# Squares of four row tiles written into PSUM banks instead of activation tiles, in a Hymba-style decoder layer

## The chip, the cores and the metric

The kernel runs on one core of a Trainium2 chip. The metric is the device time of one execution in microseconds (us). A core has five engines that run beside each other: PE (TensorE: matmuls and weight loads), DVE (VectorE), ACT (ScalarE), POOL (GpSimd) and SP (SyncE, which here issues most of the DMAs). Tiles lie in SBUF or, for what PE produces, in eight PSUM banks of 128 partitions by 512 fp32 values.

## The reference

One layer of a hybrid decoder: 256 tokens of width 2048, all in fp32.

```python
u = rmsnorm(h, ln1)
# one projection, then an RG-LRU group (8 blocks) and a retention group (8 heads)
h = h + concat(A, B) @ W_out                         # 2048 -> 2048
u = rmsnorm(h, ln2)
ff = silu(u @ w_ffn_gate) * (u @ w_ffn_up)           # 2048 -> 5632, twice
h = h + ff @ w_ffn_down                              # 5632 -> 2048
return rmsnorm(h, final_norm_w)
```

The last norm needs the sum of the squares of every row of the final `h` (2048 values of each of 256 tokens). That sum is what the changed lines compute for the left half of the columns.

## The kernel before, in words

**Arithmetic.** Every fp32 product is made of three matmuls of a rounded type: each operand is split into a high part (a cast on ACT, line 123: `wh`, `bh`, `ah`, `sh`) and a rest (a subtraction on DVE, line 124: `wl`, `bl`, `al`, `sl`), and `three` (lines 683 to 685) issues high times high, high times low and low times high. A weight block that comes in by DMA is a tile `raw` of 128x1024; splitting it costs one cast and one subtraction of that size.

**Blocks and quads.** The feed-forward part runs in blocks. Each of the two down blocks (`down_block(0)` and `down_block(1)`) produces 1024 of the 2048 output columns, as four sums `c11`, `c12`, `c21`, `c22` (first digit: token half `t`, second digit: column half), one PSUM bank each. It goes through 22 quads, each a pair of 128-row slices of the inner dimension against a 2x2 arrangement of weights `b11, b12, b22, b21`. A plain quad takes eight products (24 matmuls). A summed quad takes seven, in Strassen's manner: `p1, p5, p6, p7` go into banks of their own, and DVE first forms sums of the raw weights (line 661, four 128x512 additions in place) that are split once more as `t1, t3` and `t2, t4`. In a summed quad `b11` is split into activation tiles (`bh`, `bl`) and not into weight tiles. Block 0 ends with its last two quads taken bank by bank; the quads of block 1 begin with 0 (plain), 12 (summed), 1 (plain), 19 (summed).

**Activation tiles.** `act_tile` hands out 128x512 tiles from one pool of 60 (`acts`, `bufs=60`). A request waits until some tile of the pool is no longer read by anyone. The left operands of the down blocks, `dl[i]`, live in this pool from the beginning of block 0 to their use in block 1: `ah` and `al` for each of 22 quads, and `sh` and `sl` for those whose quad is summed. At the start of block 1, `sh` and `sl` are still needed for nine quads (5, 7, 9, 11, 12, 13, 15, 17, 19), and for two of these, 12 and 19, they lie in another pool (`BESIDE`).

**PSUM.** Two pools of four banks, `bank` and `aux`; `room` gives one to the `c` sums and the other to the `p` sums of a block, and block by block they change places. Block 0 has its four `c` in `bank`, block 1 its four `c` in `aux` and its `p` in `bank`: the banks in which the `c` of block 0 stand are those of the `p` of block 1.

**After a sum.** When a `c` of block 0 is complete, DVE adds it to the residual rows (`htok`, line 945), and `down_post` squares the rows on ACT with an accumulated sum per row (line 983). The square itself, `junk`, is read by nobody; the accumulated sum `ssq` is what is kept. For these tiles a multiplication by the norm's weight (line 988, DVE) follows, deferred by 13 to 16 steps of the program.

**Order.** The kernel is written as a list of steps, with loads three half quads ahead. A planner puts the instructions of all engines into queues by its own timeline: an instruction goes into its engine's queue when its operands and the tiles it needs are free in that plan, the earlier one in the program first. On the chip each engine's queue is then fixed. Only the last step of block 1 has its PE order written out by hand.

Of the kernel before, what the change touches and what calls it, by code (L numbers as in the profile page):

```python
# [45 lines left out]
def tile_hymba_layer(ctx: ExitStack, tc: tile.TileContext, A: dict, out: bass.AP):  # L46
# [18 lines left out]
    def nm(s):  # L65
        counter[0] += 1
        return f"{s}_{counter[0]}"

    def act_tile(name, dt=F32):
        return apool.tile([P, 512], dt, tag="act", name=nm(name))  # L70
# [169 lines left out]
    def defer(steps, f):  # L240
        later.append([steps, f])
# [664 lines left out]
    def make_left(p):  # L906
        if dl[p] is None:
            place = sum_tile if p in BESIDE else act_tile
            dl[p] = Left(ff[p], p in EARLY_DOWN + SUMMED_DOWN[0] + SUMMED_DOWN[1], place)

    def down_block(d, ahead):
        ps = {} if d else ahead.ps

        def tile_of(c):
            return 2 * d + int(c[2]) - 1, int(c[1]) - 1

        def into(c, a, b=None, op=ALU.add):

            h = htok[tile_of(c)]
            t = a  # L920
            if b is not None:
                t = act_tile("part")
                v.tensor_tensor(out=t, in0=a, in1=b, op=ALU.subtract)
            v.tensor_tensor(out=h, in0=h, in1=t, op=op)
            return t

        def post(c):
            if c == "p1":
                ps["a1"] = act_tile("part")
                act.copy(out=ps["a1"], in_=ps[c])  # L930
                into("c11", ps["a1"])
            elif c == "p7":
                n = act_tile("n")
                v.tensor_tensor(out=n, in0=ps["p6"], in1=ps["a1"], op=ALU.subtract)
                into("c12", n, ps["p5"])
                m = into("c21", n, ps["p7"], ALU.subtract)
                into("c22", m, ps["p5"])
            elif c[0] == "c":
                cb, t = tile_of(c)
                if d and c[:3] == "c22":  # L940
                    c0 = S * (c == "c22b")
                    down_post(cb, t, c0, S, ps[c][:, c0 : c0 + S])
                else:
                    h = htok[cb, t]
                    v.tensor_tensor(out=h, in0=ps[c], in1=h, op=ALU.add)
                    down_post(cb, t, 0, 512)

        n = FT // 2
        quads = []
        for i in ORDER_DOWN[d]:  # L950
            if d == 0 and i in EARLY_DOWN:
                quads.append(Direct(ahead.shared[EARLY_DOWN.index(i)]))
            else:
                quads.append(Quad(A["w_down"][d * n + i], i in SUMMED_DOWN[d], lambda i=i: make_left(i)))
            quads[-1].pair = i
        if d:
            quads[-1].apart = quads[-2].apart = True
        tail = [("c11", 0, 512), ("c12", 0, 512), ("c21", 0, 512)]
        def half_over():
            h = htok[3, 1][:, S:]  # L960
            act.copy(out=h, in_=ps["c22"][:, S:])
            v.tensor_tensor(out=ps["c22b"][:, S:], in0=ps["c22b"][:, S:], in1=h, op=ALU.add)

        early = {}
        if d:

            early["c22"] = lambda: v.tensor_tensor(out=ps["c22"], in0=ps["c22"], in1=htok[3, 1], op=ALU.add)
            early["c22b"] = half_over
            tail[:0] = [("c22b", S, S, slice(0, 1))]
            tail += [("c22", 0, S), ("c22b", S, S, slice(1, 4))]  # L970
        else:
            tail.append(("c22", 0, 512))

        block(NB + 2 + d, quads, dl, post, ps, tail, early=early, ordered=d == 1)

    def down_post(cb, t, c0, cw, src=None):

        h = htok[(cb, t)][:, c0 : c0 + cw]
        src = h if src is None else src
        f = fw[cb][:, c0 : c0 + cw]  # L980
        n = cb + (c0 > 0)
        j = act_tile("junk")
        act.activation(out=j[:, :cw], in_=src, func=AF.Square, accum_out=ssq[:, t, n : n + 1])
        p = pre[:, t : t + 1]
        if cb < 3:
            if cb < 2:

                defer(13 + 2 * cb + t, lambda: v.tensor_tensor(out=h, in0=h, in1=f, op=ALU.mult))
                return
            pool.tensor_tensor(out=h, in0=h, in1=f, op=ALU.mult)  # L990
            if cb == 2:
                if t == 0:
                    act.activation(out=warm, in_=ssq[:, t, n : n + 1], func=AF.Sqrt)
                v.tensor_reduce(out=p, in_=ssq[:, t, :3], axis=mybir.AxisListType.X, op=ALU.add)
                v.tensor_scalar(out=p, in0=p, scalar1=1.0 / D, scalar2=EPS, op0=ALU.mult, op1=ALU.add)
            return
        if c0 + cw < 512:
            v.tensor_scalar(out=p, in0=ssq[:, t, n : n + 1], scalar1=1.0 / D, scalar2=p, op0=ALU.mult, op1=ALU.add)
            v.tensor_tensor(out=h, in0=src, in1=f, op=ALU.mult)
            return  # L1000

        q, r, w = ssq[:, t, n : n + 1], r3[:, t : t + 1], m3[:, t : t + 1]
        act.activation(out=r, in_=q, func=AF.Sqrt, scale=1.0 / D, bias=p)
        v.tensor_scalar(out=w, in0=q, scalar1=1.0 / D, scalar2=p, op0=ALU.mult, op1=ALU.add)
        v.tensor_tensor(out=h, in0=src, in1=f, op=ALU.mult)
        v.reciprocal(out=r, in_=r)
        v.tensor_scalar(out=w, in0=w, scalar1=-0.5, scalar2=r, op0=ALU.mult, op1=ALU.mult)
        v.tensor_scalar(out=w, in0=w, scalar1=r, scalar2=1.5, op0=ALU.mult, op1=ALU.add)
        rw = rw3[:, t : t + 1]
        pool.tensor_tensor(out=rw, in0=r, in1=w, op=ALU.mult)  # L1010
        rows = out[t * P : t * P + P, :]
        for c in (0, 1, 3, 2):
            z = htok[(c, t)]
            if c == 1:
                act.activation(out=z, in_=z, func=AF.Copy, scale=rw)
            elif c == 2 and t:
                v.tensor_scalar(out=z[:, :S], in0=z[:, :S], scalar1=r, scalar2=w, op0=ALU.mult, op1=ALU.mult)
                act.activation(out=z[:, S:], in_=z[:, S:], func=AF.Copy, scale=rw)
            else:
                e = pool if c == 2 else v  # L1020
                e.tensor_scalar(out=z, in0=z, scalar1=r, scalar2=w, op0=ALU.mult, op1=ALU.mult)
            (act if c % 2 and t else nc.sync).dma_start(out=rows[:, c * 512 : c * 512 + 512], in_=z)
# [128 lines left out]
    for step, (units, run) in enumerate(program):  # L1151
        need += sum(un.n_loads for un in units)
        while done < min(len(loads), need + AHEAD):
            un, j = loads[done]
# [109 lines left out]
```

## Time and profile before

| | |
|---|---|
| time, median of 3 runs | 1084.82 us (1084.63 to 1085.21) |
| the profiled execution's own time | 1085.53 us |
| its span, first to last instruction | 1083.7 us |
| PE busy | 1072.3 us, 99% |
| DVE busy | 972.0 us, 90% |
| ACT busy | 666.9 us, 62% |
| POOL busy | 56.5 us, 5% |
| mean granted TensorE clock | 0.996 |

The profile describes one execution. A group line gives a source line, an engine, an operation, output and inputs, the count, the busy time and mean of one, and after the bar the idle time of the engine just before such instructions and what ended it. In a timeline, the row's first number is the start in us from the beginning of the span, the second the duration; what stands in brackets is how long the engine had been idle before and which instruction released it. A window row gives for each engine the busy time and the number of instructions, and then the granted clock of TensorE (1.00 is full speed), the share of the DMA engines and their rate. The chain that ended last is 94% PE.

### The profile page before, as it was taken

The numbers are of one execution on the slowest core, as the hardware profiler recorded it, in microseconds if no ns is written. First come the engines' busy times: TensorE is split into PE (matmuls) and PEld (weight loads), VectorE is DVE, ScalarE is ACT, GpSimd is POOL, SyncE is SP. The second block draws the span as 40 slices with busy tenths as digits, with TensorE's granted clock in tenths as the row PEclk, the third lists the DMA queues.
The fourth block names the chain that finished last, engine by engine and source line by source line (L and its number), as shares of the span: only waits on it lengthen the run. The fifth ranks groups of instructions, "written<-read, shape, count | busy, mean of one in ns | idle before, by whom it ended". The sixth has DMA issues, their size and how long they took to land.

```text
span 1083.7 us, 14591 instructions
## 1 busy us (share of the span) xinstructions
PE 1072.3 (99%) x5083; PEld 897.5 (83%) x5083; DVE 972.0 (90%) x1411; ACT 666.9 (62%) x951; POOL 56.5 (5%) x73
## 2 busy tenths in 40 slices
PE   9999999999999999999999999999999999999997
PEld 7888888888888888888888888888888888878886
DVE  7789889988878889989999999999999899999886
ACT  7756744468746676656656566565656666655463
POOL 0603230000000000000000000000000010000001
PEclk9999999999999999999999999999999999999998
DMA  9964574554557587677776777776777856557662
GB/s 328 351 211 154 176 252 168 181 176 165 185 194 236 188 306 277 227 242 247 257 269 229 250 262 238 265 269 227 251 249 228 273 170 219 194 174 240 208 214 78
DMA packets 71386, 244.62 MB, mean 226 GB/s; under 512 B 8208, under 2 KB 8592, under 8 KB 71312
## 3 DMA queue, kind: packets, MB, share of 16 engines
q1 hardware_dynamic: 68400, 236.34, 64.3%
q0 software_dynamic: 1472, 4.72, 1.3%
q10 hardware_dynamic: 1440, 2.62, 0.6%
q8 instruction: 40, 0.66, 0.2%
q14 instruction: 34, 0.28, 0.1%
HBM read 239.46 MB, written 4.19 MB: 225 GB/s over the span
## 4 chain that ended last, share of the span: by engine, by line
PE 94%; POOL 1%; DMA 1%; DVE 1%; issue 1%; ACT 1%; SPq 0%; POOLq 0%; ACTq 0%
PE c L683 22%; PE c L685 22%; PE c L684 22%; PE fm L194 10%; PE fm L196 5%; PE tm L174 2%; PE tm L176 2%; PE tm L175 2%; PE p L685 1%; PE p L684 1%; PE p L683 1%; POOL sumsq L310 1%; PE ft L868 1%; DMA raw<-in_w_lx 1%; DMA raw<-in_w_v 0%
## 5 line engine op out<-in xcount | busy, mean ns | idle before, releaser
L123 ACT CAST wh<-raw 128x1024 fp32r<-128x1024 f32 (+1 forms) x500 | 464.5, 960 | 321.6 <-PE c L685 127.3
L124 DVE TENSOR_TENSOR wl<-raw,wh 128x1024 fp32r<-128x1024 f32 (+1 forms) x500 | 543.1, 1114 | 73.0 <-ACT wh L123 71.2
L684 PE MATMUL c<-wl,ah 128*128 128x512 f32 x814 | 317.7, 390 | 0.0
L685 PE MATMUL c<-wh,al 128*128 128x512 f32 x814 | 314.9, 389 | 0.0
L683 PE MATMUL c<-wh,ah 128*128 128x512 f32 x814 | 276.8, 392 | 0.0
L683 PEld LDWEIGHTS c<-wh,ah 128*128 128x128 f32 x814 | 153.4, 188 | 31.8 <-ACT wh L123 0.3
L685 PEld LDWEIGHTS c<-wh,al 128*128 128x128 f32 x814 | 152.8, 188 | 31.7 <-DVE al L124 0.3
L684 PEld LDWEIGHTS c<-wl,ah 128*128 128x128 f32 x814 | 152.9, 188 | 31.3
L194 PE MATMUL fm<-u,wh 128*128 128x512 f32 x512 | 161.3, 396 | 0.0
L196 PEld LDWEIGHTS fm<-u,wl 128*128 128x128 f32 x512 | 96.0, 188 | 22.5
L196 PE MATMUL fm<-u,wl 128*128 128x256 f32 x512 | 100.9, 278 | 0.0
L661 DVE TENSOR_TENSOR raw<-raw,raw 128x512 f32<-128x512 f32 x118 | 81.1, 688 | 2.0
L661 DVE TENSOR_TENSOR raw<-raw 128x512 f32<-128x512 f32 x118 | 80.6, 686 | 1.1
L194 PEld LDWEIGHTS fm<-u,wh 128*128 128x128 f32 x512 | 78.3, 189 | 0.3
L684 PE MATMUL c<-wl,sh 128*128 128x512 f32 x194 | 75.2, 389 | 0.0
L685 PE MATMUL c<-wh,sl 128*128 128x512 f32 x194 | 74.0, 389 | 0.0
L683 PE MATMUL c<-wh,sh 128*128 128x512 f32 x194 | 68.7, 391 | 0.3 <-ACT sh L123 0.3
L175 PE MATMUL tm<-wl,u 128*128 128x512 f32 x128 | 48.8, 394 | 0.0
L176 PE MATMUL tm<-wh,u 128*128 128x512 f32 x128 | 48.5, 390 | 0.0
L174 PE MATMUL tm<-wh,u 128*128 128x512 f32 x128 | 47.1, 398 | 0.8 <-ACT u L298 0.8
L1119 POOL DMA_DIRECT2D htok<-kept_rows x8 | 4.3, 546 | 796.4 <-DVE wl L124 704.0
L683 PEld LDWEIGHTS c<-wh,sh 128*128 128x128 f32 x194 | 36.4, 188 | 8.2 <-ACT sh L123 0.7
(247 smaller groups left out, 1076.2 us busy)
## 6 DMA issues: line engine op xcount, KB each, us to landing
raw<-in_w_gu SPq DMA_DIRECT2D x216, 512.0 KB, 5.1
raw<-in_w_down SPq DMA_DIRECT2D x91, 512.0 KB, 4.8
raw<-in_w_out SPq DMA_DIRECT2D x34, 512.0 KB, 4.3
raw<-in_w_lx SPq DMA_DIRECT2D x16, 512.0 KB, 6.9
raw<-in_w_k SPq DMA_DIRECT2D x16, 512.0 KB, 3.5
raw<-in_w_q SPq DMA_DIRECT2D x16, 512.0 KB, 3.7
raw<-in_w_rg SPq DMA_DIRECT2D x16, 512.0 KB, 3.5
raw<-in_w_lg SPq DMA_DIRECT2D x16, 512.0 KB, 3.4
```

Of the source, the lines that this page charges most:

```text
L123: act.copy(out=dst_h, in_=src)
L124: v.tensor_tensor(out=dst_l, in0=src, in1=dst_h.bitcast(F32), op=ALU.subtract)
L174: pe.matmul(ps, ah, wh, start=first, stop=False)
L175: pe.matmul(ps, ah, wl, start=False, stop=False)
L176: pe.matmul(ps, al, wh, start=False, stop=last)
L194: pe.matmul(ps, wh, hl, start=n + i == 0, stop=False)
L196: pe.matmul(ps[:, :S], wl, hl[:, :S], start=False, stop=n + i == len(order) - 1)
L310: pool.tensor_tensor(out=sumsq, in0=sumsq, in1=sq, op=ALU.add)
L661: v.tensor_tensor(out=dst, in0=a, in1=b, op=ALU.add)
L683: pe.matmul(p, ah, bh, start=first, stop=False, skip_group_check=onto)
L684: pe.matmul(p, ah, bl, start=False, stop=False, skip_group_check=onto)
L685: pe.matmul(p, al, bh, start=False, stop=last, skip_group_check=onto)
```

## The change

`down_post` gets an argument `gone`. For the four `c` of block 0 the caller passes the PSUM bank that has just been added to the rows, and the square is written over that bank; for block 1 nothing changes, its squares still go into activation tiles.

```diff
                     h = htok[cb, t]
                     v.tensor_tensor(out=h, in0=ps[c], in1=h, op=ALU.add)
-                    down_post(cb, t, 0, 512)
+                    down_post(cb, t, 0, 512, gone=None if d else ps[c])
...
-    def down_post(cb, t, c0, cw, src=None):
+    def down_post(cb, t, c0, cw, src=None, gone=None):
...
-        j = act_tile("junk")
+        j = act_tile("junk") if gone is None else gone
         act.activation(out=j[:, :cw], in_=src, func=AF.Square, accum_out=ssq[:, t, n : n + 1])
```

## The prediction

> **What bounds the kernel now.** I read the page first.
>
> ```profile
> span 1083.7 us, 14591 instructions
> PE 1072.3 (99%) x5083; PEld 897.5 (83%) x5083; DVE 972.0 (90%) x1411; ACT 666.9 (62%) x951; POOL 56.5 (5%) x73
> ```
>
> PE is busy almost throughout, so only what stops or slows PE can move the time. Next, the table of 20 us windows, read for the PE column and the granted clock. Between 400 us and the tail one window falls out, and it is the one in which down block 0 hands over to down block 1 (neighbours beside it):
>
> ```profile
> 940.00:960.00 20.00, 20.00 (x90) 16.56 (x89) 18.48 (x24) 8.85 (x9) 0.00 (x0) 1.00 0.72 246
> 960.00:980.00 20.00, 18.66 (x73) 14.40 (x72) 18.15 (x26) 10.64 (x18) 0.00 (x0) 0.91 0.39 126
> 980.00:1000.00 20.00, 20.00 (x90) 16.57 (x89) 18.14 (x21) 11.83 (x13) 2.12 (x4) 1.00 0.78 266
> ```
>
> It holds 73 matmuls instead of 90. Of the 90, two began before the window, so 88 starts fill 20 us: one each 0.227 us. Then the timeline of PE at that place:
>
> ```profile
> 963.19 0.39 PE L684 MATMUL c<-wl,ah 128*128 128x512 f32 x1
> ...
> 963.65 0.39 PE L683 MATMUL p<-bh,ah 128*128 128x512 f32 x1
> ...
> 965.69 0.39 PE L683 MATMUL p<-wh,sh 128*128 128x512 f32 x1
> 966.86 0.50 PE L684 MATMUL p<-wl,sh 128*128 128x512 f32 x1 [0.79 <-DVE wl L124]
> 967.20 0.40 PE L685 MATMUL p<-wh,sl 128*128 128x512 f32 x1
> 967.70 0.50 PE L683 MATMUL p<-bh,ah 128*128 128x512 f32 x1
> 968.65 1.00 PE L683 MATMUL p<-wh,sh 128*128 128x512 f32 x2 [0.45 <-ACT wh L123]
> ...
> 972.62 0.39 PE L684 MATMUL p<-wl,sh 128*128 128x512 f32 x1
> ...
> 973.78 0.39 PE L684 MATMUL c<-wl,ah 128*128 128x512 f32 x1
> ```
>
> From 965.69 to 973.78 there are 19 steps from start to start. At 0.227 us they would take 4.31 us; they take 8.09. **The loss is 3.77 us**, in two parts. The steps up to 968.65 (four of them, 0.91 us) take 2.96 us: 2.05 us in which PE waits for DVE's `wl`, ACT's `bh` and ACT's `wh`. The rest, 1.7 us, is the clock, in the windows of 2 us:
>
> ```profile
> 968.00:970.00 2.00, 1.55 (x5) 1.08 (x5) 2.00 (x4) 2.00 (x3) 0.00 (x0) 0.73 0.62 234
> 970.00:972.00 2.00, 2.00 (x6) 1.52 (x5) 2.00 (x3) 1.53 (x2) 0.00 (x0) 0.50 0.24 78
> 972.00:974.00 2.00, 2.00 (x9) 1.64 (x8) 2.00 (x4) 0.00 (x0) 0.00 (x0) 0.92 0.89 258
> ```
>
> 2 x (0.27 + 0.50 + 0.08) = 1.70 us of full speed were not granted: about 3.4 us at half rate, right behind the waits.
>
> Who was late? The waits of the last 300 us and ACT's timeline name it:
>
> ```profile
> ACT junk L983 <- PE c L684: 6.2, 1, 6.2
> ```
>
> ```profile
> 955.20 0.62 ACT L123 CAST bh<-raw 128x512 fp32r<-128x512 f32 x1 [0.49 <-DVE part L923]
> 956.41 1.05 ACT L123 CAST wh<-raw 128x1024 fp32r<-128x1024 f32 x1 [0.59 <-PE c L685]
> 963.62 0.63 ACT L983 ACTIVATE junk<-htok 128x512 f32<-128x512 f32 x1 [6.16 <-PE c L684]
> 964.16 0.19 ACT L983 ACTIVATION_READ_ACCUMULATOR junk<-htok 128x1 f32 x1
> 964.25 1.04 ACT L123 CAST wh<-raw 128x1024 fp32r<-128x1024 f32 x1
> ...
> 967.04 0.60 ACT L123 CAST bh<-raw 128x512 fp32r<-128x512 f32 x1
> 967.55 4.03 ACT L123 CAST wh<-raw 128x1024 fp32r<-128x1024 f32 x4
> ```
>
> The square of `c11` stands at the head of ACT's queue from 957.46 to 963.62, and the casts behind it with it. It waits for a matmul of line 684 that reads `ah`: the one that starts at 963.19 and ends at 963.58, the last use of quad 0's `ah`. That fits a count of the activation tiles in the code: `ah` and `al` of 22 quads (44) and `sh`, `sl` of seven (14) are 58 of 60; the other two go to quad 12's `bh` (955.20, freed by a `part`) and its `bl`. No sixty-first tile exists until quad 0 is through.
>
> **The change part by part.** It removes four requests for an activation tile; it adds no instruction, no DMA and no step, and four banks are now written once more.
>
> *The squares themselves.* No row shows a square into PSUM. The nearest are a copy from SBUF to PSUM (line 811) and the square as it is:
>
> ```profile
> L983 ACT ACTIVATE junk<-htok 128x512 f32<-128x512 f32 x7 | 4.4, 626 | 10.6 <-PE c L684 6.2 <-DVE htok L945 4.4
> ...
> L811 ACT COPY c<-q 128x512 f32<-128x512 f32 x2 | 1.2, 582 | 1.3 <-DVE q L810 1.3
> ```
>
> So between 44 ns less and no difference for each, at most 0.18 us for four, on an engine that was idle for 6.16 us there. I take nothing.
>
> *The banks are held longer.* DVE's rows at this place:
>
> ```profile
> 957.05 1.29 DVE L945 TENSOR_TENSOR htok<-c,htok 128x512 f32<-128x512 f32 x2 [0.15 <-PE c L685]
> ...
> 960.59 0.68 DVE L945 TENSOR_TENSOR htok<-c,htok 128x512 f32<-128x512 f32 x1
> ...
> 961.90 1.42 DVE L661 TENSOR_TENSOR raw<-raw,raw 128x512 f32<-128x512 f32 x2
> 964.38 0.69 DVE L988 TENSOR_TENSOR htok<-htok,fw 128x512 f32<-128x512 f32 x1 [1.06 <-ACT junk L983]
> 964.99 0.69 DVE L661 TENSOR_TENSOR raw<-raw 128x512 f32<-128x512 f32 x1
> 965.59 1.22 DVE L124 TENSOR_TENSOR wl<-raw,wh 128x1024 fp32r<-128x1024 f32 x1
> 966.73 1.89 DVE L988 TENSOR_TENSOR htok<-htok,fw 128x512 f32<-128x512 f32 x3
> ...
> 969.14 1.22 DVE L124 TENSOR_TENSOR wl<-raw,wh 128x1024 fp32r<-128x1024 f32 x1
> ...
> 970.87 2.35 DVE L124 TENSOR_TENSOR wl<-raw,wh 128x1024 fp32r<-128x1024 f32 x2
> ```
>
> The first two sums are added by 958.3, the last by 961.27; with a square of 0.63 and its read of 0.19 us behind each, the last bank is free by 962.1 instead of 961.3. The next user of any of the four is a `p` of quad 12, the first one at 963.65, the second bank at 965.69, the others later; by 963.65 all four are free. This costs nothing as long as the four squares stand ahead of later casts in ACT's queue; what it costs if they don't is the third rival. The Trainium skill, page "PSUM — Partial Sum Buffer", section "Summary: rules for kernel authors", advises to evacuate banks promptly, which speaks against the change: by it every bank is kept 0.8 us longer, and with a PE that waited for banks the sum would lose up to that much per bank. By the rows above nobody waits for a bank, so it leaves the sum as it is.
>
> *ACT's queue.* Without the wait the four squares run at the adds' pace (957.7 to 962.1), and the cast of quad 12's `t1, t3` (964.25 before) can start when DVE's second addition of line 661 is done, 962.6. What is late next? The shortage itself stays: the next request for an activation tile is quad 19's `bh` (967.04 before), and it now inherits quad 0's `ah` at 963.58. If it stands in the queue ahead of the cast of `t1, t3`, that cast starts at 963.62 + 0.53 = 964.15, as late as before; but everything behind is three squares (1.83 us) and more earlier, and PE first needs this `bh` for the matmul of 967.70, at full rate three steps behind 965.69: 966.37.
>
> *DVE becomes the pace.* Its rows leave no gap from 964.38 to 973.2, and the only idle time the change gives back is the 1.06 us before line 988. So with the same order each later `wl` ends 1.06 us earlier. PE at full rate from 965.69 needs:
> - the `wl` of `t1, t3` at 965.92; it ended at 966.81, now 965.75: in time.
> - the `wl` of `t2, t4` (969.14 + 1.22 = 970.36, now 969.30) for the matmul of 972.62, 14 steps on: 968.87. Late by 0.43.
> - the first of the two `wl` at 970.87 (ends 972.05 at the latest, now 970.99) for the matmul of 973.78, 19 steps on: 970.01. **Late by 0.98.**
>
> What follows has more room. So 0.98 of the 3.77 us stay as a wait, provided that the clock holds: a gain of **2.8 us**. The bounds come from where the planner puts the four multiplications of line 988 (0.63 us each), which can now start early. If the three of 966.73 go behind the needed subtractions, nothing is late and the gain is 3.77. If all four go ahead of the first `wl`, that ends at 965.75 + 1.89 = 967.64 against 965.92, 1.72 late, and the gain is 2.05.
>
> *After 975 us.* PE has no further wait up to the tail (each window to 1060 us shows 20.00), and the row of 980 to 1000 shows DVE at 18.14 of 20 us: it catches up 1.9 us in each 20. So the gain should be carried to the end. The tail behind the last matmul uses none of the changed lines.
>
> The sum: the profiled execution took 1085.53 us; less 2.8 it would be 1082.7 (span 1080.9). It lies 0.71 above the median 1084.82, from which the forecast is made: **1082.0 us**, 1081.1 to 1082.8 for this case alone.
>
> **The rivals.** *First: the clock drops all the same.* The trace shows half rate after 2.05 us of waiting in pieces within 3 us; the case above leaves 1.0 to 1.7 us in pieces within 5. If that suffices, 1.7 us are lost again and the gain is 0.35 to 1.1: 1083.7 to 1084.5, centre 1084.1. For it: the place and kind of wait are the same, DVE stays behind. Against: the only other gap of PE between 60 us and the tail, 0.30 us, left the clock at 1.00:
>
> ```profile
> 360.00:380.00 20.00, 19.70 (x86) 1.00 0.57 186
> ```
>
> (columns here: length, PE, clock, DMA.) It is far shorter, so it weighs little. The Trainium skill, page "TensorE: Matmul & The Clock Gate", section "Part 1: The HAM clock gate", has the array at half rate after at least one idle window of about 3.4 us. The length agrees with the 3.4 us found here, the condition doesn't: PE was never idle that long. Taken literally the rule would rule this rival out; by the trace it stays.
>
> *Second: the change doesn't do what it says.* The wait goes over whole to the cast of quad 19's `bh`, with the cast of `t1, t3` and the squares' successors in the same order behind it, and DVE gains nothing because it waits for that cast: 1084.8. For it: the pool is as full as before. Against: the 1.06 us of DVE hung on the square, not on a cast, and three squares are gone from between.
>
> *Third: slower.* The planner puts quad 19's `bh` ahead of the squares. Then ACT stands until 963.62 as before; the `bh` ends at 964.2, the four squares (0.61 us each) at 966.6, and only then come the banks and the cast of `t1, t3` (967.65), its `wl` 968.9. The first `p` matmul waits for its bank from 963.65 to 964.8 (1.15 us), and the one that needs this `wl` from 967.1 to 968.9 (1.8 us): 2.95 us instead of 2.05, and with waits spread over 5 us two stretches of half rate (3.4 us instead of 1.7). 2.6 us slower, 1087.4. It decides at the order of the squares and this `bh` in ACT's queue. Against it: the squares come earlier in the program, and their operands were there by 961.27, before a tile is free.
>
> **How the numbers follow.** Forecast 0.58, first rival 0.22, second 0.08, third 0.12. With three runs of this kernel 0.2% (2.17 us) is about what can be told from no change: below 1082.65 is faster, which takes nearly all of the forecast's case; the first two rivals are no change. Faster 0.58, same 0.30, slower 0.12. The range leaves out the third rival and the far ends: from 1080.8 (the full 3.77, the squares' 0.18, the spread of runs) to 1085.2 (the second rival with the spread shown).
>
> **What would show it.** Right: no wait of line 983 for `PE c L684`, the four squares between 957 and 962.5; the 6 us gone or shorter and named at a `bh` of line 123; the window 960 to 980 with 80 or more matmuls and a clock near 1.00. Wrong step by step: PE waiting for ACT's squares at a `p` (banks); half rate still there although PE's waits are under 1.7 us (first rival); waits later than 980 us that before doesn't have (the gain given back).

## The result, and the profile after

The changed kernel is **slower**: 1089.0 us, median of 5 runs (1088.61 to 1090.24), beside 1084.92 us (1084.63 to 1085.23) for the kernel before. The ratio is 1.0043, with a 95% interval of 1.0032 to 1.0054. The forecast was 1082.0 us; the measured time lies 3.8 us above the upper end of the range. One run below, of `after_turn_first`, was far slower than its nine others (2196.96 us) and is left out of its median.

The profiled execution took 1090.16 us. Its span, from the page, and its windows of 20 us (columns as in the prediction):

```profile
span 1088.4 us, 14591 instructions
```

```profile
960.00:980.00 20.00, 17.69 (x70) 13.72 (x69) 17.97 (x25) 9.98 (x14) 0.00 (x0) 0.91 0.32 106
980.00:1000.00 20.00, 18.42 (x78) 14.14 (x78) 13.84 (x15) 8.31 (x10) 2.13 (x4) 1.00 0.69 227
1000.00:1020.00 20.00, 19.95 (x88) 15.99 (x87) 17.49 (x20) 10.74 (x12) 0.00 (x0) 1.00 0.60 197
1020.00:1040.00 20.00, 20.00 (x88) 16.00 (x87) 16.84 (x21) 10.95 (x12) 0.00 (x0) 1.00 0.62 201
1040.00:1060.00 20.00, 20.00 (x89) 16.25 (x88) 17.14 (x21) 12.08 (x14) 0.00 (x0) 1.00 0.68 218
```

Two things have happened. The window of the hand-over, which was to go from 73 matmuls to 80 or more, has gone to 70. And the stretch behind it, 980 to 1060 us, which had 90 in each window before, has lost 12, 2, 2 and 1. At 0.227 us each the 17 + 3 matmuls are 4.5 us; the span is 4.7 us longer.

For all that follows one figure is taken from each profiled execution: the sum, over all steps from one matmul's start to the next, of what a step exceeds 0.24 us. It is 3.59 us for the kernel before in 960 to 980 us (the prediction counted 3.77 against 0.227 us) and 0.00 in 980 to 1060. For the changed kernel it is **4.35 and 3.51 us**. The net difference is 4.27 us; the medians differ by 4.1.

**The squares did what the prediction said.** ACT's timeline of the changed kernel (start, duration; in brackets the idle time before and what ended it):

```profile
958.09 0.60 ACT L983 ACTIVATE c<-htok 128x512 f32<-128x512 f32 x1 [0.56 <-DVE htok L945]
...
961.62 0.60 ACT L983 ACTIVATE c<-htok 128x512 f32<-128x512 f32 x1 [0.47 <-DVE htok L945]
...
963.69 0.63 ACT L123 CAST bh<-raw 128x512 fp32r<-128x512 f32 x1 [1.34 <-PE c L684]
965.28 1.06 ACT L123 CAST wh<-raw 128x1024 fp32r<-128x1024 f32 x1 [0.97 <-DVE raw L661]
968.83 1.99 ACT L123 CAST wh<-raw 128x1024 fp32r<-128x1024 f32 x2 [2.49 <-DVE raw L661]
```

The wait of 6.16 us is gone; the four squares run from 958.09 to 962.22 and wait only for the additions in front of them. The shortage has passed to quad 19's `bh`, as forecast, and costs ACT 1.34 us there. But the cast of `t1, t3` starts at 965.28, a microsecond *later* than before (964.25), and what ended the idle time before it is DVE. Here is DVE:

```profile
961.50 1.28 DVE L988 TENSOR_TENSOR htok<-htok,fw 128x512 f32<-128x512 f32 x2
962.71 0.68 DVE L661 TENSOR_TENSOR raw<-raw 128x512 f32<-128x512 f32 x1
963.31 1.28 DVE L988 TENSOR_TENSOR htok<-htok,fw 128x512 f32<-128x512 f32 x2
964.51 0.68 DVE L661 TENSOR_TENSOR raw<-raw,raw 128x512 f32<-128x512 f32 x1
965.12 0.68 DVE L124 TENSOR_TENSOR bl<-raw,bh 128x512 fp32r<-128x512 f32 x1
965.72 0.68 DVE L661 TENSOR_TENSOR raw<-raw,raw 128x512 f32<-128x512 f32 x1
966.32 0.68 DVE L661 TENSOR_TENSOR raw<-raw 128x512 f32<-128x512 f32 x1
966.92 1.22 DVE L124 TENSOR_TENSOR wl<-raw,wh 128x1024 fp32r<-128x1024 f32 x1
968.06 0.68 DVE L661 TENSOR_TENSOR raw<-raw 128x512 f32<-128x512 f32 x1
```

All four multiplications of line 988 now stand in front of the second addition of line 661. That addition ends at 965.19; the cast of `t1, t3` needs the first two additions and starts 0.09 us later. Behind it stands quad 19's `bl`, and behind that two more additions, so that the `wl` of `t1, t3` ends at 968.14 (before: 966.81). The last row is the addition that ACT's next cast, at 968.83, waited 2.49 us for. That cast is of `t2, t4`, so this row is quad 12's fourth addition, and the one of the same form at 966.32 is quad 19's first, which has gone ahead of it (before the change quad 12's stood at 964.99 and quad 19's at 970.27). PE pays for both:

```profile
968.20 0.50 PE L684 MATMUL p<-wl,sh 128*128 128x512 f32 x1 [1.31 <-DVE wl L124]
...
969.93 0.73 PE L683 MATMUL p<-wh,sh 128*128 128x512 f32 x2 [1.00 <-ACT wh L123]
```

Half rate follows again, in 970 to 974 us, (0.35 + 0.50) x 2 = 1.70 us of full speed not granted, as much as before. Of the 4.35 us the two waits, with the steps right behind them, are 2.87 and the steps at half rate 1.48. The same view shows PE idle for 0.96 us in 994 to 996 with the clock untouched, to which the last section comes back:

```profile
966.00:968.00 2.00, 0.89 (x4) 0.36 (x3) 2.00 (x3) 0.34 (x1) 0.00 (x0) 1.00 0.00 0
968.00:970.00 2.00, 0.81 (x3) 0.37 (x3) 1.44 (x4) 1.17 (x2) 0.00 (x0) 1.00 0.39 113
970.00:972.00 2.00, 2.00 (x6) 1.61 (x7) 2.00 (x2) 2.00 (x3) 0.00 (x0) 0.65 0.37 150
972.00:974.00 2.00, 2.00 (x6) 1.52 (x5) 2.00 (x3) 0.71 (x1) 0.00 (x0) 0.50 0.87 240
...
994.00:996.00 2.00, 1.04 (x3) 0.59 (x4) 1.28 (x2) 2.00 (x3) 0.00 (x0) 1.00 0.62 238
```

**The second loss is 25 us later.** ACT in the kernel before, and then ACT, DVE and PE in the changed one:

```profile
983.95 1.05 ACT L123 CAST wh<-raw 128x1024 fp32r<-128x1024 f32 x1 [0.94 <-PE c L685]
985.18 0.62 ACT L123 CAST bh<-raw 128x512 fp32r<-128x512 f32 x1 [0.17 <-DMA raw<-in_w_down]
988.78 4.02 ACT L123 CAST wh<-raw 128x1024 fp32r<-128x1024 f32 x4 [2.98 <-PE c L685]
```

```profile
987.26 0.62 ACT L123 CAST bh<-raw 128x512 fp32r<-128x512 f32 x1 [5.45 <-DMA raw<-in_w_down]
...
993.65 3.90 ACT L123 CAST wh<-raw 128x1024 fp32r<-128x1024 f32 x4 [3.86 <-PE p L685]
```

```profile
987.91 0.69 DVE L124 TENSOR_TENSOR bl<-raw,bh 128x512 fp32r<-128x512 f32 x1 [4.27 <-ACT bh L123]
```

```profile
994.75 0.50 PE L683 MATMUL p<-wh,sh 128*128 128x512 f32 x1 [1.18 <-ACT wh L123]
```

This `bh` is quad 7's. In ACT's order before it stands behind two casts of quad 5, which start there at 981.96 and 983.95; in the new order it stands in front of them (the row of 987.26; they follow at 987.79), and it waits 5.45 us for its load with those casts behind it (before: 0.17 us). DVE stands 4.27 us at its `bl` meanwhile, and PE pays 1.18 us at 994.75 and smaller sums from 990 to 1048 us. Nothing that the diff touches runs there: it is the planner's order that has changed.

### The profile page after: what moved, and what is told of

The parts are those of the page before. It is cut to its first block, busy times and chain, and to the rows that moved or that the text cites. A ratio compares the mean times of both kernels' runs of the same rounds, so it can differ in the third digit from the quotient of the medians.

```text
span 1088.4 us, 14591 instructions
## 1 busy us (share of the span) xinstructions
PE 1073.6 (99%) x5083; PEld 896.1 (82%) x5083; DVE 972.2 (89%) x1411; ACT 666.1 (61%) x951; POOL 55.8 (5%) x73
## 4 chain that ended last, share of the span: by engine, by line
PE 90%; DVE 4%; issue 1%; POOL 1%; DMA 1%; ACT 1%; SPq 0%; POOLq 0%; ACTq 0%; DVEq 0%
PE c L683 21%; PE c L684 21%; PE c L685 21%; PE fm L194 10%; PE fm L196 5%; PE tm L174 3%; PE tm L176 3%; PE tm L175 3%; DVE wl L124 2%; POOL sumsq L310 1%; DVE raw L661 1%; DMA raw<-in_w_down 1%; PE ft L868 1%; PE p L685 1%; PE p L684 1%
```

## The experiments

"Loss" is the sum defined above, in us, from one profiled execution each. Ratios are against the kernel before, run on the same chip.

| kernel | loss 960 to 980 | loss 980 to 1060 | median, us | ratio, 95% interval |
|---|---|---|---|---|
| before | 3.59 | 0.00 | 1084.2 to 1084.9 | |
| after | 4.35 | 3.51 | 1089.0 | 1.0043, 1.0032 to 1.0054 |
| after_mul_late | 1.00 | 1.20 | 1083.44 | 0.9992, 0.9983 to 1.0001 |
| after_mul_between | 2.06 | 1.06 | 1083.9 | 0.9992, 0.9983 to 1.0001 |
| before_mul_late | 2.56 | 1.09 | 1084.84 | 1.0000, 0.9992 to 1.0009 |
| after_mul_pool | 2.21 | 0.63 | 1084.78 | 1.0001, 0.9992 to 1.0010 |
| after_mul_tail | 0.99 | 0.00 | 1082.54 | 0.9984, 0.9975 to 0.9993 |
| before_mul_tail | 1.85 | 0.00 | 1083.65 | 0.9995, 0.9987 to 1.0004 |
| after_bh_in_turn | 1.47 | 0.00 | 1083.12 | 0.9989, 0.9979 to 0.9998 |
| after_mul_two | 2.13 | 3.26 | 1086.49 | 1.0018, 1.0009 to 1.0027 |
| after_turn_later | 4.12 | 0.00 | 1084.29 | 1.0003, 0.9994 to 1.0012 |
| after_turn_first | 2.04 | 2.66 | 1086.0 | 1.0012, 1.0002 to 1.0021 |
| before_turn | 3.59 | 0.00 | 1084.3 | 0.9997, 0.9988 to 1.0006 |
| **after_tail_turn** | **0.00** | **0.00** | **1081.17** | **0.9971, 0.9960 to 0.9981** |

The first column can hold two places: in the kernels before and after all of it lies before 974.2 us, but in `after_mul_late` and `after_mul_tail` 0.71 us of it lie at 977 to 980, in `before_mul_tail` 0.65 and in `before_mul_late` 1.36, mainly in waits for casts of ACT.

Line numbers lie 2 to 15 higher in some of these kernels. `issue_after(x)` tells the planner to put what follows no earlier than the instruction `x`.

**Are the multiplications of line 988 the cause?** The first four runs move them. In `after_mul_late` they come behind the last subtraction written so far, which puts them at 1014 to 1033 us; `before_mul_late` does the same to the kernel before.

```diff
+        last_low[0] = v.tensor_tensor(out=dst_l, in0=src, in1=dst_h.bitcast(F32), op=ALU.subtract)
...
-                defer(13 + 2 * cb + t, lambda: v.tensor_tensor(out=h, in0=h, in1=f, op=ALU.mult))
+                def weigh():
+                    with tc.issue_after(last_low[0].ins):
+                        v.tensor_tensor(out=h, in0=h, in1=f, op=ALU.mult)
+
+                defer(13 + 2 * cb + t, weigh)
```

> The changed kernel with the four multiplications of line 988 queued on DVE behind a subtraction that belongs to a load 13 to 16 steps later. Theory 1 (the loss comes from these four multiplications, 2.5 us of DVE work that the planner now puts ahead of the additions that feed ACT's cast of t1, t3): the second addition is back at about 962, the cast at 964.2 behind quad 19's bh, the first wl ends near 967.2; PE loses under 1.2 us instead of 4.5 at the hand-over and nothing at 990, so about 1081.5 to 1083. Theory 2 (squares into the PSUM banks hurt by themselves, by writes into PSUM beside matmuls or banks given back late): PE still loses at the hand-over, 1087 or more. Theory 3 (the stall at 990 to 996 is a separate effect of the new order of casts): the hand-over heals and 990 doesn't, about 1085.

> The kernel before (squares in activation tiles, so ACT still waits until 963.6 for quad 0's ah) with only the multiplications of line 988 queued late, as in the first of these runs. Theory 1: DVE loses its wait of 1.06 us and 2.5 us of work at the hand-over, so part of the 3.77 us comes back though ACT's wait stays: 1082 to 1084. If ACT's wait was the whole cause of the stall: 1084.8, as before.

The hand-over loss falls from 4.35 to 1.00 us, and only to 2.56 in the kernel before, where the square still stands 6.15 us in ACT's queue; up to 970 us alone it is 0.29 and 1.20. But 1.1 to 1.2 us come back where the multiplications now stand, among the additions and subtractions of other summed quads, and neither kernel's time differs clearly from the kernel before.

`after_mul_between` puts the multiplications back where the prediction assumed them: the first multiplication between the third and the fourth addition of quad 12, the other three behind its first subtraction.

```diff
+            if getattr(self, "pair", None) == 12:
+                marks[:] = last_sum[-2], last_low[0]
...
+                    with tc.issue_after(marks[bool(cb or t)].ins):
+                        v.tensor_tensor(out=h, in0=h, in1=f, op=ALU.mult)
```

> The changed kernel with the multiplications of line 988 put on DVE where they stood before the change: one behind the third addition of quad 12, three behind the subtraction of t1, t3. This is the order on which the prediction's 2.8 us rest. Theory 1: the gain predicted, 1081 to 1083, with waits of PE of about 1 us at the hand-over and no half clock. Theory 1b (DVE has no room at all at this place, wherever the multiplications stand before 973): later subtractions are late instead, the clock drops, about 1084 to 1085. Theory 2 (PSUM): 1087 or more.

The loss is 2.06 us, not 0.98; 1.48 of it lie up to 970 us, the rest at 979 to 980. So with the multiplications in their old places the sum of the prediction would still have been about 0.5 us short at the hand-over, since the rest of DVE's order isn't the old one: quad 19's `bl` stands ahead of quad 12's fourth addition, and DVE stands for its cast first (0.36 us); and quad 19's first addition, the second row, stands ahead of the `wl` of `t2, t4`, for which PE waits until 969.85. The 1.06 us behind 980 come without multiplications there; no run isolates their cause.

```profile
963.82 0.69 DVE L126 TENSOR_TENSOR bl<-raw,bh 128x512 fp32r<-128x512 f32 x1 [0.36 <-ACT bh L125]
...
967.98 0.68 DVE L665 TENSOR_TENSOR raw<-raw 128x512 f32<-128x512 f32 x1
```

`after_mul_pool` gives the multiplications to POOL.

```diff
-                defer(13 + 2 * cb + t, lambda: v.tensor_tensor(out=h, in0=h, in1=f, op=ALU.mult))
+                defer(13 + 2 * cb + t, lambda: pool.tensor_tensor(out=h, in0=h, in1=f, op=ALU.mult))
```

> The changed kernel with the four multiplications of line 988 on POOL instead of DVE (two such on POOL take 1.27 us each at the end of the kernel). DVE's order at the hand-over is then the same as with the multiplications held back. Theory 1: as with the multiplications late, 1081.5 to 1083; up to 1 us more if POOL's work beside DVE slows DVE's rows. Theory 2: 1087 or more.

No gain on the kernel before: DVE is slower beside them. POOL's timeline, then DVE's:

```profile
958.67 7.16 POOL L988 TENSOR_TENSOR htok<-htok,fw 128x512 f32<-128x512 f32 x4 [67.21 <-ACT c L983]
```

```profile
960.08 1.19 DVE L124 TENSOR_TENSOR bl<-raw,bh 128x512 fp32r<-128x512 f32 x1
961.18 0.68 DVE L945 TENSOR_TENSOR htok<-c,htok 128x512 f32<-128x512 f32 x1
961.79 1.18 DVE L661 TENSOR_TENSOR raw<-raw 128x512 f32<-128x512 f32 x1
963.00 3.37 DVE L661 TENSOR_TENSOR raw<-raw,raw 128x512 f32<-128x512 f32 x2
```

The subtraction and the first addition take 1.19 and 1.18 instead of 0.68 us, the next two additions 3.37 instead of 1.42: 2.95 us more on DVE, beside 2.5 us that were taken off it. The addition at 961.18, which reads one operand from PSUM, isn't slowed.

**What part of it are they, and what is the rest?** In `after_mul_tail` the multiplications go behind additions near the end of block 1, where they meet no quad; `before_mul_tail` is the same edit of the kernel before. `after_mul_two` sends only the two of token half 1 there.

```diff
+    def behind(ins, n):
+        with tc.issue_after(ins.ins):
+            for f in waiting[:n]:
+                f()
+        del waiting[:n]
...
+            behind(v.tensor_tensor(out=ps["c22b"][:, S:], in0=ps["c22b"][:, S:], in1=h, op=ALU.add), 2)
...
-                defer(13 + 2 * cb + t, lambda: v.tensor_tensor(out=h, in0=h, in1=f, op=ALU.mult))
+                waiting.append(lambda: v.tensor_tensor(out=h, in0=h, in1=f, op=ALU.mult))
```

> The changed kernel with the four multiplications of line 988 moved to the tail, between DVE's last additions, where DVE has gaps of 0.8 to 1.1 us. The hand-over should look as with the multiplications held back (gaps of PE beyond its normal step of about 1.0 us in 960 to 980 instead of 4.4 in the changed kernel), and the 1.2 us of gaps that the held-back multiplications made at 1010 to 1040, where they then stood, should be gone: about 1.2 us under that run, 1082 to 1082.5. If those late gaps have another cause they stay, and it is 1083.4 again. If four multiplications don't fit in the tail's gaps, the tail grows by up to 2.5 us: 1084 or more.

> The kernel before, squares in activation tiles, with the four multiplications in the tail. With them held back to 1014 to 1032 it lost 2.6 us in 960 to 980, where ACT's wait stays, and 1.0 at 1030 to 1040. If the multiplications were the cause of the later 1.0, about 1083.5 to 1084 here. The difference to the changed kernel with the multiplications in the tail is what the change is worth by itself: about 1.5 us if the theory holds that ACT's wait costs PE 1 to 2 us, nothing if it doesn't matter.

> The changed kernel with two of the four multiplications (first token half) left where the planner puts them, ahead of the additions, and two in the tail. If each multiplication ahead of the additions costs PE its 0.63 us, the gaps of PE in 960 to 980 lie halfway between the 1.0 us of none and the 4.4 of four: 2 to 3.5 us, depending on whether the clock drops. Time about 1083 to 1085.5. If only their order against one addition matters, it is at either end.

With the multiplications out of the way the change gains: 1082.54 us, and 1.1 us less than the same edit gives to the kernel before, which keeps the wait. ACT's row in the waits of `before_mul_tail`, 955 to 980 us (total, times, longest):

```profile
ACT junk L993 <- PE c L684: 6.2, 1, 6.2
```

PE in `after_mul_two`:

```profile
966.96 0.50 PE L684 MATMUL p<-wl,sh 128*128 128x512 f32 x1 [0.61 <-DVE wl L124]
...
968.69 0.73 PE L683 MATMUL p<-wh,sh 128*128 128x512 f32 x2 [1.00 <-ACT wh L123]
```

With half of the multiplications PE's first wait falls from 1.31 to 0.61 us. The second stays at 1.00: it comes from quad 12's fourth addition, which stands behind the first `wl` here too. No half rate follows in this execution. So 2.13 beside 4.35 us isn't a halving of the waits; most of the difference is the clock. The later loss is 3.26 us with two multiplications ahead, 3.51 with four and 0.00 with none (`after_mul_tail`). It doesn't grow in step with them; the next runs show that it depends on which order comes out.

`after_bh_in_turn` leaves the multiplications where the change put them and holds back, in block 1, each summed quad's `bh` and `bl` until the cast of the previous summed quad's `t1, t3` is placed.

```diff
-                split(*self.parts["b11"], r[:, :512])
+                with tc.issue_after(summed_high[0].ins) if self.half and summed_high[0] else ExitStack():
+                    split(*self.parts["b11"], r[:, :512])
...
             self.cut(("t1", "t3"), self.ra)
+            if self.half:
+                summed_high[0] = last_high[0]
```

> The changed kernel, multiplications of line 988 untouched, but in down block 1 each cast of bh is queued on ACT behind the cast of t1, t3 of the summed quad before it. In the changed kernel quad 7's bh stood ahead of two casts of quad 5 and waited 5.45 us for its load, and PE lost some 3 us between 988 and 1010. If that order is the cause of the second loss, it goes and the hand-over's loss stays: about 1086. If the second loss only follows from loads that came late because DVE was late at the hand-over, it stays: 1088 to 1089.

The time is 1083.12 us where about 1086 was expected: the edit removes the later loss wholly and two thirds of the first, 1.48 us of this by the half rate, which doesn't come. DVE and ACT:

```profile
963.96 1.41 DVE L666 TENSOR_TENSOR raw<-raw,raw 128x512 f32<-128x512 f32 x2
...
966.01 1.22 DVE L126 TENSOR_TENSOR wl<-raw,wh 128x1024 fp32r<-128x1024 f32 x1
```

```profile
964.75 1.05 ACT L125 CAST wh<-raw 128x1024 fp32r<-128x1024 f32 x1 [2.96 <-DVE raw L666]
965.71 0.61 ACT L125 CAST bh<-raw 128x512 fp32r<-128x512 f32 x1
```

ACT still waits 2.96 us, since the multiplications still stand ahead of the additions; but `bh` comes behind the cast, `bl` no longer stands ahead of the first `wl`, and that ends at 967.23 instead of 968.14.

The next two runs split this edit: `after_turn_later` leaves quad 19 out of it, `after_turn_first` holds back quad 19 alone. `before_turn` is the whole edit on the kernel before.

```diff
-... if self.half and summed_high[0] else ExitStack():
+... if self.half and summed_high[0] and self.pair != 19 else ExitStack():
```

> The changed kernel with the bh casts in turn from quad 5 on; quad 19's bh and all four multiplications stay where the planner put them, so DVE's queue is that of the changed kernel up to quad 19's subtractions. Theory A (two losses, each with its own cause): the hand-over loses 2.4 us of waits, and 1.9 more if the clock drops, and nothing is lost after 985: 1083 to 1085. Theory B (the later loss only follows from the hand-over): some 3 us are lost after 985 again, 1088.

> The changed kernel with only quad 19's bh behind quad 12's cast of t1, t3; the later bh casts stay ahead, as the planner puts them. Theory A: the hand-over loses about 1.5 us, as with all bh in turn, and 2.5 to 3.5 us are lost between 985 and 1050, where bh waits for its load: 1085 to 1087. Theory B: no late loss, 1083.

> The kernel before with only the bh casts in turn. ACT's wait for quad 0's ah stays, and so does the hand-over's loss of 3.6 us (1.7 of it where the clock drops); nothing was lost behind it. So no difference, 1084.3. If it is much faster, the order of the bh casts and not the wait for a tile was the cause of the loss before, too.

Windows of `after_turn_later`, then of `after_turn_first`:

```profile
960.00:980.00 20.00, 17.88 (x71) 14.02 (x70) 19.02 (x26) 10.62 (x14) 0.00 (x0) 0.91 0.39 131
980.00:1000.00 20.00, 20.00 (x90) 16.57 (x89) 18.36 (x20) 11.31 (x12) 2.12 (x4) 1.00 0.77 264
```

```profile
960.00:980.00 20.00, 19.20 (x82) 14.79 (x80) 18.52 (x26) 10.13 (x14) 0.00 (x0) 1.00 0.41 130
...
1000.00:1020.00 20.00, 19.22 (x82) 15.04 (x82) 16.49 (x20) 10.95 (x12) 0.00 (x0) 1.00 0.63 208
```

The two losses come apart. Holding back the later quads removes the later one and leaves the first (71 matmuls, 4.12 us); holding back quad 19 brings the first down to 2.04 us, at a clock of 1.00, and leaves 2.66 us of the later one. The kernel before gains nothing from it (0.9997).

**Both mends together.** `after_tail_turn` is the change with the edit of `after_mul_tail` and that of `after_bh_in_turn`.

> The changed kernel with both mends: multiplications of line 988 in the tail and the bh casts in turn. With the multiplications in the tail alone 1.0 us of gaps were left (0.3 at 960 to 970, 0.7 at 970 to 980). If those come from bh casts that wait at the head of ACT's queue, 0.3 or less is left: 1081.8 to 1082.3, the fastest of all. If not, 1082.5 again.

```profile
960.00:980.00 20.00, 20.00 (x90) 16.57 (x89) 19.56 (x23) 12.45 (x16) 0.76 (x2) 1.00 0.50 167
980.00:1000.00 20.00, 20.00 (x90) 16.57 (x89) 18.07 (x21) 11.01 (x13) 1.36 (x3) 1.00 0.80 271
```

```profile
963.23 1.22 DVE L126 TENSOR_TENSOR wl<-raw,wh 128x1024 fp32r<-128x1024 f32 x1
```

PE has no gap left at the hand-over, the first `wl` ends at 964.45, and the kernel takes 1081.17 us: 3.7 us less than the kernel before beside it (1084.83), about the whole 3.59 us that the hand-over cost. It beats both kernels. The squares still go into PSUM here, so that they cost PE nothing by themselves. The two mends without the change were each run (1083.65 and 1084.3), not together, so how much of the 3.7 us needs the change isn't shown; with the multiplications in the tail the change is worth 1.1 us.

The two mends make a table of four for the loss in 960 to 980 us: neither 4.35, `bh` in turn 1.47, multiplications away 0.99, both 0.00. Each mend alone also ends the half rate in its profiled execution (clock 1.00 in 960 to 980). The parts don't add up place by place: the whole 4.35 lie before 974.2, but 0.71 of the 0.99 lie at 977 to 980. So both orders have a part in the loss, and how the two share it isn't isolated.

## Why the prediction was wrong

- **What bounds the kernel, and the 3.77 us: right.** With the waits gone, the median falls by 3.7 us (`after_tail_turn`), though by what the last section says of the clock the 3.77 us are those of an execution of the rarer kind.
- **The squares and the banks: right.** 0.58 to 0.60 us each instead of 0.626, at 958.09 to 962.22 (957.7 to 962.1 said); no matmul waits for a bank.
- **The wait of ACT: right.** It is gone and quad 19's `bh` inherits the tile, starting at 963.69 (963.58 said).
- **"So with the same order each later `wl` ends 1.06 us earlier": the failed step.** The order on DVE didn't stay: all four multiplications, quad 19's `bl` and quad 19's first addition went ahead of the first `wl`, and quad 12's fourth addition went behind it. That the multiplications went ahead because the squares no longer wait in the planner's timeline is argued; that timeline isn't on record. The prediction did see the four multiplications, as a bound: three more of 0.63 us ahead of the first `wl` end it at 967.64. It ended at 968.14, `bl` being ahead as well, and PE's wait for it, 1.31 us, is within the bound's 1.72. What was in no part of the sum is the cast of `t2, t4`: it waits 2.49 us for the addition that went behind, and PE stands for another 1.00 us. With the half rate the loss at the hand-over is 4.35 us instead of 0.98, or of the bound's 1.72.
- **"So the gain should be carried to the end": the second failed step.** It rested on the windows of the kernel before, which have room for DVE in the order of before. The new order puts quad 7's `bh`, whose load hadn't come, ahead of two casts of quad 5: 3.51 us with the smaller sums behind it. Waits later than 980 us were the last of the prediction's own signs of being wrong. With this, 4.35 + 3.51 against 3.59 gives the 4.27 us of the profiled runs.
- **The rivals.** The first (the clock) did happen in the profiled run, but on longer waits than the 1.0 to 1.7 us that it speaks of; at waits of that size, in `after_mul_between` (loss up to 970 us 1.48) and `after_bh_in_turn` (1.47), the clock stayed at 1.00. The second didn't happen. The third had the sign, but its mechanism (`bh` ahead of the squares, banks waited for) is not what the trace shows: the squares stand first, and no bank is waited for. That its chance of 0.12 was on "slower" is luck. The prediction asked after the order of ACT around one instruction, after that of DVE only for a bound on one `wl`, and for the 80 us behind not at all.

## What to carry to other kernels

Where a planner writes the order of the queues, taking away a wait changes the order of everything behind it: work of no urgency (here 2.5 us of multiplications) is ready early and goes ahead of the chain that feeds TensorE. List, for each engine, what becomes ready earlier by the edit and what stands behind it, before costing the edit by the old order; and read a changed trace far beyond the place of the edit. The edit and the order have to be mended together: here the edit alone costs 4.1 us, and the edit with two constraints on the order is 3.7 us faster than the kernel before.

## What the runs showed of the hardware

**Equal waits don't always bring half rate.** In the changed kernel PE stood 1.11 + 1.19 = 2.30 us in 966 to 970, and half rate followed. In `after_mul_pool` it stood 0.93 + 0.76 = 1.69 us in the same 4 us, and it didn't:

```profile
966.00:968.00 2.00, 1.07 (x4) 0.48 (x3) 2.00 (x4) 0.33 (x1) 0.00 (x0) 1.00 0.00 0
968.00:970.00 2.00, 1.24 (x5) 1.05 (x6) 2.00 (x4) 2.00 (x3) 0.00 (x0) 1.00 0.00 0
970.00:972.00 2.00, 2.00 (x10) 1.51 (x9) 2.00 (x2) 1.68 (x2) 0.00 (x0) 1.00 0.78 260
```

That alone could be a threshold. But the kernel before, by the same count, stood 0.89 us in this row and 0.45 in that of 968 to 970 (shown in the prediction), 1.34 together, and half rate followed:

```profile
966.00:968.00 2.00, 1.11 (x4) 0.48 (x3) 2.00 (x4) 2.00 (x6) 0.00 (x0) 1.00 0.13 29
```

And the second stall of the changed kernel, 1.58 us in 980 to 1000, left the clock at 1.00. So the length of the waits doesn't decide alone; what else does wasn't isolated.

The record shows that it differs from one execution to the next. Four profiled executions have half rate at the hand-over (`before`, `after`, `before_turn`, `after_turn_later`), each with 1.70 to 1.72 us of full speed not granted, and these four have a mean granted clock of 0.996; the other ten have 0.997 to 0.999. If 0.996 is taken as the sign of it, which is an estimate, it came in 25 of the 95 executions of the kernel before that ran beside the experiments, in all 5 of the changed kernel, in 2 of 10 of `after_turn_later`, in 3 of 11 of `after_mul_pool` and in none of `after_mul_between` (11), `after_bh_in_turn` (10) and `after_tail_turn` (7). The 25 took 1085.1 us on average, the other 70 1084.3: it makes an execution some 0.8 us longer, not 1.70. The profiled execution of the kernel before, with its loss of 3.59 us, is one of the rarer kind.

The Trainium skill, page "TensorE: Matmul & The Clock Gate", section "Part 1: The HAM clock gate (the "warmup" mystery)", says that the gate's window is free-running, so that the point of transition varies with where in it the first matmul lands. That one kernel's executions differ fits this. The runs don't agree with the condition the page gives for half rate, an idle window of about 3.4 us, since no wait of PE at the hand-over or in the second stall is longer than 1.31 us.

**POOL beside DVE.** Instructions of DVE with two operands in SBUF took up to 2.4 times their time (3.37 against 1.42 us) beside POOL's multiplications, and the one with an operand in PSUM took its usual 0.68. The Trainium skill, page "SBUF — State Buffer", section "SBUF: two separate sides", has these two engines share a pair of ports as an exclusive lock, which DVE needs for two SBUF inputs against a GpSimd instruction that reads SBUF, as the multiplications do. The rows agree on which instructions are slowed; whether a lock slows them or a shared rate, they don't show.
